# A one-core hybrid decoder layer: other load prices for the planner, small inverses head by head, one chain of k norms per head, and a new layout of the final norm

## The chip, the cores and the metric

One core of a Trainium2 chip runs the whole kernel. The metric is the device time of one execution in microseconds (us); the kernel before was run three times. The engines are TensorE (PE), VectorE (DVE), ScalarE (ACT), GpSimd (POOL) and SyncE (SP); SP issues all loads and stores here. PSUM has eight banks of 512 float32 columns, into which PE writes.

## What is computed

One layer and a final norm, batch 1, 1024 tokens, width 1024, all float32:

```python
h = rmsnorm(x, norm_mix_w);  proj = h @ W_in
qkv = silu(causal_conv4(qkv));  q, k = l2norm(q), l2norm(k)      # 4 heads of 128
o = gated_delta_rule_chunked(q, k, v, g, beta)                   # chunks of 64, I + A solved per chunk
gdn_out = rmsnorm(o) * silu(z)
lru_out = rg_lru(causal_conv4(lru_x)) * gelu(lru_gate)           # 512 channels, gates, scan over tokens
x = x + concat(gdn_out, lru_out) @ W_out
u = relu(rmsnorm(x) @ W1);  x = x + (u * u) @ W2                 # 4096 wide
return rmsnorm(x, final_norm_w)
```

## The kernel before

Activations are kept transposed, features on the partitions and tokens along the free axis, in two halves of 512 tokens. Each float32 product is three matmuls of split operands (`mm3`, line 439: high by high, high by low, low by high), so an operand costs a cast on ACT (the high part) and a subtraction on DVE (the low part).

**Stages.** PE works through: the first tiles with the input norm and the gates (to 45 us); the 28 tiles of the input projection, with the delta rule's heads and the recurrent unit's groups strewn between them (the mixer, to 408 us); the output projection (to 488); the first feed-forward product as seven Winograd products per pair of blocks (to 795); and the second, which has the four stages of `STAGES` (line 1250), products (1, 7), (6, 5), (2, 4) and (3). A stage walks over 16 column blocks in pairs; for each block `get2` (line 1263) loads tiles of W2 (`w2r`) and of the stored activations (`ur`), combines and splits them, and `mm3` adds to the stage's PSUM banks `p2`, eight for a stage of two products. At the end of a stage DVE or ACT reads each bank into the running sums `p1`, `u2`, `u3`, `p5`.

**Heads.** When a head's q and k tiles are there, `after_tile` (line 1028) records `decay`, `gd_k` (684) and `gd_q` (717) for each half: decay rows `DT` from a load `qg<-gcd`, the k norms (`sk`, `rk`, `cj`), the products `psA` and from them `U`. `invert32(h)` (739) then inverts the 32 x 32 diagonal blocks: SP copies U's blocks to DRAM and back as `N` (bn, N), POOL runs 31 steps of two operations (`tm`, `V`), SP copies the result to `Y` (bv, Y). `gd_inv` and `gd_scan` use it.

**Tail.** `normed` (1317) makes the final norm: sums of squares by matmuls into bank `n3p`, an inverse square root by `rsqrt` (485: a bit trick and three Newton steps on DVE), the factor broadcast to all partitions by PE into `n3b`, then a multiply for each of eight tiles into `ot`, and the store. It is called once for tokens 0 to 511, and for the other half in two quarters of 256 tokens (`end=True`), whose last products have 256 columns.

**Order.** Nothing runs as it is written. Every call is recorded as an operation with a due time (`pl.at`, `chain`) in the class `Plan`. `emit` (280) then plays the operations through with prices (`price`, 259): at each step it takes the operation that could start first, earliest due time first among those that can, and writes it to its engine. That fixes each engine's order, and it also fixes which buffer a tile gets: of the 84 slabs of 128 x 512 and of the eight banks, the one that in the played time came free last before the start. A real operation then waits for whichever engine last used that buffer. A load's price is its bytes at a rate, plus a constant to landing; `SLACK` is added before a mixer matmul counts as ready. Since all instructions are written out by one statement, all have the line L370.

```python
r.slot = max((x for x in sl if x[0] <= s), default=min(sl))
...
if e == "sy":
    free[e] = s + 0.45
    dma = max(dma, free[e] + 0.65) + c
    o.end = dma + 0.95
```

Of the kernel before, what the change touches and what calls it, by code (L numbers as in the profile page):

```python
# [9 lines left out]
AF = mybir.ActivationFunctionType  # L10
# [23 lines left out]
SLACK = 1.5  # L34
# [145 lines left out]
class Plan:  # L180
# [78 lines left out]
    def price(e, method, args, kw):  # L259
# [6 lines left out]
        if e == "sy":  # L266
            return n * shape[0] * 4 / 360e3
# [10 lines left out]
        return 0.15 + 0.0021 * n  # L278

    def emit(self, engines, caps):  # L280
# [62 lines left out]
        for _ in range(len(ops)):  # L343
# [15 lines left out]
            if e == "sy":  # L359
                free[e] = s + 0.45  # L360
                dma = max(dma, free[e] + 0.65) + c
                o.end = dma + 0.95
# [22 lines left out]
def layer(ctx: ExitStack, tc: tile.TileContext, xT, win, wba, prm, cst, wga, wgx, wout, w1, w2, out):  # L385
# [80 lines left out]
    gp.memset(onesd, 1.0 / D)  # L466
    with pl.at(due=-5000.0):
        ac.activation(out=one("load", [P, 1]), in_=onesd, func=AF.Exp)
# [16 lines left out]
    def rsqrt(y, x):  # L485

        t = small("rst", [P, 4], 3)[:, 0:x.shape[-1]]
        ve.tensor_scalar(out=y.bitcast(I32), in0=x.bitcast(I32), scalar1=1, scalar2=None, op0=ALU.logical_shift_right)
        ve.tensor_scalar(out=y.bitcast(I32), in0=y.bitcast(I32), scalar1=-1.0, scalar2=float(0x5f3759df), op0=ALU.mult, op1=ALU.add)
        for _ in range(3):  # L490
            ve.tensor_mul(out=t, in0=y, in1=y)
            ve.scalar_tensor_tensor(out=t, in0=t, scalar=-0.5, in1=x, op0=ALU.mult, op1=ALU.mult)
            ve.scalar_tensor_tensor(out=y, in0=t, scalar=1.5, in1=y, op0=ALU.add, op1=ALU.mult)
# [190 lines left out]
    def gd_k(h, hf):  # L684
        S = HD[h]
        c4 = slice(hf * 4, hf * 4 + 4)
# [7 lines left out]
        sk, cj = S["sk"][:, c4], S["cj"][:, c4]  # L694
        for c in range(4):
            cc = slice(c * P, (c + 1) * P)
            ac.activation(out=small("osq", [P, P], 2), in_=psK[:, cc], func=AF.Square, accum_out=S["sk"][:, hf * 4 + c:hf * 4 + c + 1])
            ac.activation(out=kd[:, cc], in_=psK[:, cc], func=AF.Copy, scale=d[:, c, P - 1:P])
        ve.tensor_scalar_add(out=sk, in0=sk, scalar1=EPS)
        rk = small("rk", [P, 4])  # L700
        rsqrt(rk, sk)
        ve.tensor_mul(out=cj, in0=rk, in1=G["beta"][:, h, c4])
        ve.tensor_mul(out=cj, in0=cj, in1=rk)
        ve.tensor_mul(out=sk, in0=sk, in1=rk)

        psA = bank("psA")
        with pl.unit(0.86):
            for c in range(4):
                ks = slice(c * P, (c + 1) * P)
                pe.matmul(psA[:, ks], lhsT=kT[:, ks], rhs=kT[:, ks], start=True, stop=True)  # L710
        U = S["U"][hf]
        for c in range(4):
            n = hf * 4 + c
            ve.scalar_tensor_tensor(out=U[:, c * P:(c + 1) * P], in0=psA[:, c * P:(c + 1) * P], scalar=S["cj"][:, n:n + 1],
                                    in1=S["DT"][hf][:, c * P:(c + 1) * P], op0=ALU.mult, op1=ALU.mult)

    def gd_q(h, hf):
# [16 lines left out]
        pn = S["pn"][:, hf * 4:hf * 4 + 4]  # L734
        for c in range(4):
            ac.activation(out=small("osq", [P, P], 2), in_=psQ[:, c * P:(c + 1) * P], func=AF.Square, accum_out=pn[:, c:c + 1])
        ve.tensor_scalar(out=pn, in0=pn, scalar1=EPS, scalar2=EPS * P, op0=ALU.add, op1=ALU.mult)
# [780 lines left out]
```

## Time and profile before

| | |
|---|---|
| runs, us | 1141.26, 1143.0, 1137.72; median 1141.26 |
| profiled execution | 1138.41 us, its span 1136.4 us (2.0 us lie around it) |
| PE busy | 1098.7 us, 97% of the span |
| DVE, ACT, POOL busy | 864.9 us (76%), 561.9 us (49%), 98.2 us (9%) |
| mean granted PE clock | 0.985 of full speed |

An engine's busy share is an average over stages. PE is pipelined, so a stretch of starts without gaps tells more than a busy time; a timeline row gives the start, the duration and, in brackets, the idle time ahead of it with what ended it.

### The profile page before, as it was taken

How to read it: one execution, taken by the hardware profiler on the slowest of the kernel's cores; microseconds unless marked ns; L12 is line 12 of the kernel's file. 1: busy time of each engine (PE TensorE's matmuls, PEld its weight loads, DVE VectorE, ACT ScalarE, POOL GpSimd, SP SyncE). 2: the span in 40 equal slices, each digit the busy share in tenths (PEclk: the TensorE clock that was granted, in tenths of full speed). 3: DMA queues.
4: the chain of work that ended last, by engine and by line, in shares of the span. 5: the costliest groups of instructions: out<-in, count | busy, mean ns of one | idle time of the engine just before them, and what ended most of it. 6: DMA issues, size and time to landing. Idle time of an engine off the chain costs nothing.

```text
span 1136.4 us, 16117 instructions
## 1 busy us (share of the span) xinstructions
PE 1098.7 (97%) x5439; PEld 903.7 (80%) x5439; DVE 864.9 (76%) x1730; ACT 561.9 (49%) x1143; POOL 98.2 (9%) x285
## 2 busy tenths in 40 slices
PE   9999899999999999999999999999999999799994
PEld 7788678787787878888888888888888788688884
DVE  7978486786769686698978788888765756865886
ACT  8578446354475865554333333334445434554432
POOL 0004826125000000000000000000000000000001
PEclk9999899999999999999999999999999999899997
DMA  6122312121111034424443434446755455476454
GB/s 232 38 72 60 93 41 68 28 62 40 46 37 38 19 129 147 150 93 167 176 175 131 166 141 159 147 158 222 242 193 200 154 178 204 162 237 210 166 177 149
DMA packets 88098, 150.79 MB, mean 133 GB/s; under 512 B 22312, under 2 KB 25040, under 8 KB 88016
## 3 DMA queue, kind: packets, MB, share of 16 engines
q1 hardware_dynamic: 88016, 149.77, 38.6%
q8 instruction: 43, 0.70, 0.3%
q14 instruction: 39, 0.32, 0.1%
HBM read 110.91 MB, written 38.82 MB: 132 GB/s over the span
## 4 chain that ended last, share of the span: by engine, by line
PE 75%; DVE 8%; POOL 8%; issue 3%; ACT 2%; DMA 2%; SPq 1%; DVEq 0%; POOLq 0%
PE p L370 27%; PE pf L370 27%; PE pj L370 8%; PE po L370 7%; POOL V L370 4%; POOL tm L370 4%; SPq L370 1%; DVE y L370 1%; PE pvs L370 1%; DVE ig L370 1%; ACT L370 1%; PE psr L370 1%; DVE ss L370 1%; PE psZ L370 1%; PE psO L370 1%
## 5 line engine op out<-in xcount | busy, mean ns | idle before, releaser
L370 PE MATMUL pj<-xh,w 128*128 128x512 f32 x704 | 248.4, 408 | 1.4 <-DVE S L370 0.7
L370 PEld LDWEIGHTS pj<-xh,w 128*128 128x128 f32 x704 | 133.7, 190 | 29.4 <-DVE S L370 1.1
L370 PE MATMUL pj<-xl,w 128*128 128x512 f32 x352 | 138.5, 394 | 0.0
L370 PE MATMUL po<-mxh,w 128*128 128x512 f32 x256 | 79.3, 390 | 0.4 <-ACT mxh L370 0.4
L370 DVE TENSOR_TENSOR w<-r,w 128x512 fp32r<-128x512 f32 (+1 forms) x62 | 59.0, 951 | 26.2 <-ACT w L370 25.8
L370 ACT ACTIVATE c<-c 128x512 f32<-128x512 f32 x64 | 40.1, 630 | 74.0 <-DVE c L370 74.0
L370 DVE SCALAR_TENSOR_TENSOR y<-p,pr,y 128x512 f32<-128x512 f32 (+3 forms) x96 | 72.0, 754 | 5.3 <-ACT y L370 4.4
L370 ACT CAST w<-r 128x512 fp32r<-128x512 f32 (+1 forms) x62 | 51.4, 830 | 49.1 <-PE pf L370 29.0
L370 POOL TENSOR_TENSOR r<-p__9746,n3rb 128x256 f32<-128x256 f32 x2 | 1.9, 974 | 850.8 <-DMA outT<-r 850.8
L370 PEld LDWEIGHTS pj<-xl,w 128*128 128x128 f32 x352 | 67.1, 190 | 10.2
L370 PEld LDWEIGHTS po<-mxh,w 128*128 128x128 f32 x256 | 48.0, 188 | 10.7 <-ACT mxh L370 0.8
L370 POOL TENSOR_TENSOR tm<-V,N 128x60 f32<-128x60 f32 (+24 forms) x124 | 43.6, 354 | 145.1 <-DMA N<-bn 110.0
L370 PE MATMUL po<-mxl,w 128*128 128x512 f32 x128 | 49.9, 390 | 1.2 <-DVE mxl L370 1.2
L370 POOL TENSOR_TENSOR V<-V,tm 128x60 f32<-128x60 f32 (+24 forms) x124 | 44.9, 365 | 8.3
L370 DVE SCALAR_TENSOR_TENSOR c<-c,n2B 128x512 f32<-128x512 f32 x64 | 43.7, 689 | 0.5
L370 ACT ACT_TABLE_LOAD x31 | 39.8, 1283 | 6.3 <-DVE y L370 3.7
L370 PE MATMUL pf<-B5h,w 128*128 128x512 f32 x128 | 42.4, 391 | 0.0
L370 PE MATMUL pf<-B6h,w 128*128 128x512 f32 x128 | 42.0, 389 | 0.0
L370 DVE TENSOR_TENSOR c<-pf,u 128x512 f32<-128x512 f32 x48 | 32.8, 688 | 0.8 <-PE pf L370 0.4
L370 PE MATMUL p<-u2h,v2h 128*128 128x512 f32 x64 | 25.8, 403 | 7.0 <-ACT u4h L370 7.0
L370 DVE TENSOR_TENSOR s<-w2r,s 128x512 f32<-128x512 f32 x16 | 11.1, 691 | 26.5 <-DMA w2r<-w 26.5
L370 PEld LDWEIGHTS po<-mxl,w 128*128 128x128 f32 x128 | 24.0, 188 | 6.5 <-DVE mxl L370 1.5
(513 smaller groups left out, 3025.6 us busy)
## 6 DMA issues: line engine op xcount, KB each, us to landing
w2r<-w SPq DMA_DIRECT2D x112, 256.0 KB, 3.4
ur<-ud SPq DMA_DIRECT2D x112, 256.0 KB, 5.1
r<-w SPq DMA_DIRECT2D x32, 512.0 KB, 3.6
ud<-c SPq DMA_DIRECT2D x64, 256.0 KB, 2.0
ud<-ut SPq DMA_DIRECT2D x48, 256.0 KB, 2.1
r<-win SPq DMA_DIRECT2D x22, 512.0 KB, 3.7
xraw<-xT SPq DMA_DIRECT2D x16, 256.0 KB, 5.3
r<-wout SPq DMA_DIRECT2D x8, 512.0 KB, 4.4
```

Source lines behind the costliest of these rows:

```text
L370: getattr(engines[e], method)(*[v.ap() if isinstance(v, View) else v for v in args], **{k: v.ap() if isinstance(v, View) else v for k, v i ...
```

## The change

- The planner's prices: a load's bytes at 300 instead of 360 GB/s, 2.0 us to landing instead of 0.95, a POOL operation 0.05 us dearer, a slack of 1.0 instead of 1.5 us. All orders, slabs and banks come out anew.
- `gd_k` makes no norms; a new `gd_u(h)` makes one chain for both halves of a head (8 columns), then both `psA` and `U`. The q sums get their addition once per head.
- `invert32(h)` may start only after the last POOL operation of head h-1's inverse.
- Final norm, both quarters: Sqrt on ACT with a bias and a DVE reciprocal and one Newton step in place of bit trick and three steps; an early Sqrt (`root`) on a scalar tile; the multiplies read the bank `n3b` itself, all on DVE, without ACT's copy `n3rb` and POOL's share. Outputs go through slabs in place of two buffers of 128 x 1024. The sum of squares of the finished tiles stands second in the list instead of first, and all eight last banks take block 14 first and then block 15.

```diff
--- before.py
+++ after.py
@@ -31,7 +31,8 @@
 LOOK = 4
-SLACK = 1.5
+SLACK = 1.0
+LAND = 2.0
 EPS = 1e-6
@@ -264,7 +265,7 @@
         if e == "sy":
-            return n * shape[0] * 4 / 360e3
+            return n * shape[0] * 4 / 300e3
         psum = any(v.root.tag == "m" for v in src)
@@ -275,7 +276,7 @@
             return 0.036 + 0.00083 * n
-        return 0.15 + 0.0021 * n
+        return 0.2 + 0.0021 * n
 
@@ -359,7 +360,7 @@
                 dma = max(dma, free[e] + 0.65) + c
-                o.end = dma + 0.95
+                o.end = dma + LAND
             else:
@@ -464,6 +465,8 @@
     gp.memset(onesd, 1.0 / D)
+    eps = one("eps", [P, 1])
+    gp.memset(eps, EPS)
     with pl.at(due=-5000.0):
@@ -484,13 +487,16 @@
 
-        t = small("rst", [P, 4], 3)[:, 0:x.shape[-1]]
         ve.tensor_scalar(out=y.bitcast(I32), in0=x.bitcast(I32), scalar1=1, scalar2=None, op0=ALU.logical_shift_right)
         for _ in range(3):
-            ve.tensor_mul(out=t, in0=y, in1=y)
-            ve.scalar_tensor_tensor(out=t, in0=t, scalar=-0.5, in1=x, op0=ALU.mult, op1=ALU.mult)
-            ve.scalar_tensor_tensor(out=y, in0=t, scalar=1.5, in1=y, op0=ALU.add, op1=ALU.mult)
+            newton(y, x)
+
+    def newton(y, x):
+        t = small("rst", [P, NC], 3)[:, 0:x.shape[-1]]
+        ve.tensor_mul(out=t, in0=y, in1=y)
+        ve.scalar_tensor_tensor(out=t, in0=t, scalar=-0.5, in1=x, op0=ALU.mult, op1=ALU.mult)
+        ve.scalar_tensor_tensor(out=y, in0=t, scalar=1.5, in1=y, op0=ALU.add, op1=ALU.mult)
 
@@ -683,7 +689,6 @@
         S = HD[h]
-        c4 = slice(hf * 4, hf * 4 + 4)
         d = b3(S["DT"][hf])
@@ -691,28 +696,33 @@
         kd = S["kd"][hf] = slab("kd")
-        sk, cj = S["sk"][:, c4], S["cj"][:, c4]
         for c in range(4):
             ac.activation(out=kd[:, cc], in_=psK[:, cc], func=AF.Copy, scale=d[:, c, P - 1:P])
+
+    def gd_u(h):
+
+        S = HD[h]
+        sk, cj = S["sk"], S["cj"]
         ve.tensor_scalar_add(out=sk, in0=sk, scalar1=EPS)
-        rk = small("rk", [P, 4])
+        rk = small("rk", [P, NC])
         rsqrt(rk, sk)
-        ve.tensor_mul(out=cj, in0=rk, in1=G["beta"][:, h, c4])
+        ve.tensor_mul(out=cj, in0=rk, in1=G["beta"][:, h, :])
         ve.tensor_mul(out=cj, in0=cj, in1=rk)
         ve.tensor_mul(out=sk, in0=sk, in1=rk)
-
-        psA = bank("psA")
-        with pl.unit(0.86):
+        for hf in range(2):
+            kT = store[4 + h, hf]
+            psA = bank("psA")
+            with pl.unit(0.86):
+                for c in range(4):
+                    ks = slice(c * P, (c + 1) * P)
+                    pe.matmul(psA[:, ks], lhsT=kT[:, ks], rhs=kT[:, ks], start=True, stop=True)
+            U = S["U"][hf]
             for c in range(4):
-                ks = slice(c * P, (c + 1) * P)
-                pe.matmul(psA[:, ks], lhsT=kT[:, ks], rhs=kT[:, ks], start=True, stop=True)
-        U = S["U"][hf]
-        for c in range(4):
-            n = hf * 4 + c
-            ve.scalar_tensor_tensor(out=U[:, c * P:(c + 1) * P], in0=psA[:, c * P:(c + 1) * P], scalar=S["cj"][:, n:n + 1],
-                                    in1=S["DT"][hf][:, c * P:(c + 1) * P], op0=ALU.mult, op1=ALU.mult)
+                n = hf * 4 + c
+                ve.scalar_tensor_tensor(out=U[:, c * P:(c + 1) * P], in0=psA[:, c * P:(c + 1) * P], scalar=cj[:, n:n + 1],
+                                        in1=S["DT"][hf][:, c * P:(c + 1) * P], op0=ALU.mult, op1=ALU.mult)
 
@@ -731,10 +741,12 @@
                 pe.transpose(psQ[:, c * P:(c + 1) * P], qT[:, c * P:(c + 1) * P], ident)
-        pn = S["pn"][:, hf * 4:hf * 4 + 4]
+        pn = S["pn"]
         for c in range(4):
-            ac.activation(out=small("osq", [P, P], 2), in_=psQ[:, c * P:(c + 1) * P], func=AF.Square, accum_out=pn[:, c:c + 1])
-        ve.tensor_scalar(out=pn, in0=pn, scalar1=EPS, scalar2=EPS * P, op0=ALU.add, op1=ALU.mult)
+            n = hf * 4 + c
+            ac.activation(out=small("osq", [P, P], 2), in_=psQ[:, c * P:(c + 1) * P], func=AF.Square, accum_out=pn[:, n:n + 1])
+        if hf == 1:
+            ve.tensor_scalar(out=pn, in0=pn, scalar1=EPS, scalar2=EPS * P, op0=ALU.add, op1=ALU.mult)
 
@@ -764,6 +776,7 @@
             gp.tensor_tensor(out=V[:, 0:r, m + 1:], in0=V[:, 0:r, m + 1:], in1=tv, op=ALU.subtract)
+        S["inv"] = pl.ops[-1]
         bv = pl.tile(dpool, [32, 8, 4, 32], F32, "bv", "bv", True)
@@ -1039,6 +1052,8 @@
                     with pl.at(due=t, gate=HD[h]["rowop"][1]):
+                        gd_u(h)
+                    with pl.at(due=t, gate=HD[h - 1]["inv"] if h else HD[h]["rowop"][1]):
                         invert32(h)
@@ -1314,7 +1329,7 @@
 
-    def normed(hf, X, parts, a, n, t, lead, end):
+    def normed(X, parts, a, n, t, lead, end):
 
@@ -1326,34 +1341,31 @@
             r, v = small("n3r", [P, 4])[:, 0:m], small("ms", [P, 4])[:, 0:m]
-            if one is not None:
+            if end:
+                for c in range(m):
+                    ac.activation(out=r[:, c:c + 1], in_=pn[c], func=AF.Sqrt, bias=eps)
+                    ve.tensor_scalar_add(out=v[:, c:c + 1], in0=pn[c], scalar1=EPS)
+                ve.reciprocal(out=r, in_=r)
+                newton(r, v)
+            else:
                 ve.tensor_scalar_add(out=v, in0=one[:, 0:m], scalar1=EPS)
-            else:
-                for c in range(m):
-                    ve.tensor_scalar_add(out=v[:, c:c + 1], in0=pn[c], scalar1=EPS)
-            rsqrt(r, v)
+                rsqrt(r, v)
             pb = bank("n3b")
                 rows(pb, r, m)
-            if end:
-                rb = slab("n3rb")[:, 0:n]
-                ac.copy(out=rb, in_=pb[:, 0:n])
-            g = T // n
+            g = 512 // n
             for j, d in enumerate(lead):
                 if j % g == 0:
-                    ot = raw_t("ot")
+                    ot = slab("ot")
                 y = ot[:, j % g * n:j % g * n + n]
                     ve.scalar_tensor_tensor(out=y, in0=X[d], scalar=par("fnw", d), in1=pb[:, 0:n], op0=ALU.mult, op1=ALU.mult)
-                elif j in (3, 5):
-                    gp.tensor_mul(out=y, in0=X[d], in1=rb)
                 else:
-                    ve.tensor_mul(out=y, in0=X[d], in1=rb)
-                k = 1 if end and j < 2 else 2
-                if (j + 1) % k == 0:
-                    b = lead[j + 1 - k]
-                    sy.dma_start(out=out[b * P:(b + k) * P, a:a + n].rearrange("(d p) t -> p d t", p=P),
-                                 in_=ot[:, (j + 1 - k) % g * n:(j % g + 1) * n].rearrange("p (d t) -> p d t", d=k))
+                    ve.tensor_tensor(out=y, in0=pb[:, 0:n], in1=X[d], op=ALU.mult)
+                if (j + 1) % g == 0:
+                    b = lead[j + 1 - g]
+                    sy.dma_start(out=out[b * P:(b + g) * P, a:a + n].rearrange("(d p) t -> p d t", p=P),
+                                 in_=ot.rearrange("p (d t) -> p d t", d=g))
 
@@ -1427,15 +1439,17 @@
                         plus(s1, y)
-            normed(0, [p1[d] for d in range(4)] + [u3[d] for d in range(4)], [(s1, t - 40)], 0, 512, t - 30, list(range(KT)), False)
+            normed([p1[d] for d in range(4)] + [u3[d] for d in range(4)], [(s1, t - 40)], 0, 512, t - 30, list(range(KT)), False)
 
     t = ts(3, NG - 2)
+    with pl.at(due=-1000.0, gate=seen[3 * NG + 4]):
+        ac.activation(out=one("root", [P, 1]), in_=onesd, func=AF.Sqrt, bias=eps)
     with chain(t - 60):
         qs = slice(o, o + 256)
-        parts = [(ss[:, qs], t)]
+        parts = []
         xs = {}
@@ -1448,8 +1462,9 @@
                 ac.activation(out=xs[d], in_=x, func=AF.Copy, scale=par("fnw", d))
+        parts.insert(1, (ss[:, qs], t))
         X = [xs[d] for d in range(4)] + [p5[d][:, qs] for d in range(4)]
-        normed(1, X, parts, 512 + o, 256, t + o / 50, [4, 5, 6, 7, 0, 1, 2, 3], True)
+        normed(X, parts, 512 + o, 256, t + o / 50, [4, 5, 6, 7, 0, 1, 2, 3], True)
```

How the order moves, at three places. **SP in stage 2 of the second feed-forward product**, the loads of blocks 12 and 13 (a row's brackets are the semaphores it waits for: DMA queues, and the engine that last used the buffer). Before:

```order
L370 DMA w2r_9347<-w2 128x512 [waits DMAHW6_49,DMAHW5_49,DVE_49]
L370 DMA w2r_9349<-w2 128x512 [waits DMAHW7_49]
L370 DMA ur_9354<-ud12_6_7559 128x512 [waits DMAHW0_49,PE_49]
L370 DMA ur_9359<-ud12_5_7539 128x512 [waits DMAHW1_49,PE_49]
L370 DMA w2r_9361<-w2 128x512 [waits DMAHW4_49,DMAHW2_49]
L370 DMA w2r_9366<-w2 128x512 [waits DMAHW3_49]
L370 DMA ur_9371<-ud13_6_7728 128x512
L370 DMA ur_9374<-ud13_5_7708 128x512
```

Now:

```order
L371 DMA w2r_9307<-w2 128x512 [waits DMAHW6_49,PE_49]
L371 DMA w2r_9311<-w2 128x512 [waits DMAHW7_49]
L371 DMA ur_9316<-ud12_6_7520 128x512 [waits DMAHW0_49,DVE_49]
L371 DMA ur_9321<-ud12_5_7480 128x512 [waits DMAHW5_49,DMAHW1_49,DVE_49]
L371 DMA w2r_9323<-w2 128x512 [waits DMAHW2_49]
L371 DMA w2r_9328<-w2 128x512 [waits DMAHW3_49]
L371 DMA ur_9333<-ud13_6_7689 128x512 [waits DMAHW4_49]
L371 DMA ur_9335<-ud13_5_7649 128x512
```

The first w2 load of the pair waited for DVE, and the u loads for PE. Now the w2 load waits for PE, and the first two u loads for DVE.

**SP at head 1 in the mixer**: gcd loads `qg`, block copies `bn` and `N` of the inverses, W_in tiles `r`. Before:

```order
L370 DMA r_1173<-win 128x1024 [waits DMAHW4_49,Activation_49]
L370 DMA qg_1206<-gcd_708 128x512 [waits DMAHW5_49]
L370 DMA bn_1223<-U1_0_1204 32x4x32 [waits DMAHW6_49,DVE_49]
L370 DMA bn_1223<-U1_0_1204 32x4x32 [waits DMAHW7_49]
L370 DMA bn_1223<-U1_0_1204 32x4x32 [waits DMAHW0_49]
L370 DMA bn_1223<-U1_0_1204 32x4x32 [waits DMAHW1_49]
L370 DMA bn_1223<-U1_1_1309 32x4x32 [waits DMAHW2_49,DVE_49]
L370 DMA bn_1223<-U1_1_1309 32x4x32 [waits DMAHW3_49]
L370 DMA bn_1223<-U1_1_1309 32x4x32 [waits DMAHW4_49]
L370 DMA bn_1223<-U1_1_1309 32x4x32 [waits DMAHW5_49]
L370 DMA qg_1353<-gcd_708 128x512 [waits DMAHW6_49,Pool_49]
L370 DMA r_1368<-win 128x1024 [waits DMAHW7_49,Activation_49]
```

Now:

```order
L371 DMA r_1070<-win 128x1024 [waits DMAHW4_49,Activation_49]
L371 DMA N0_1107<-bn_1027 32x512 [waits DMAHW5_49,DMAHW3_49,DMAHW6_49,DMAHW2_49,DMAHW7_49,DMAHW1_49,DMAHW0_49]
L371 DMA N0_1107<-bn_1027 32x512 x3
L371 DMA N1_1138<-bn_1027 32x512 [waits DVE_49,PE_49]
L371 DMA N1_1138<-bn_1027 32x512 x2
L371 DMA N1_1138<-bn_1027 32x512 [waits DMAHW4_49]
L371 DMA qg_1165<-gcd_714 128x512 [waits DMAHW5_49]
L371 DMA qg_1231<-gcd_714 128x512 [waits DMAHW6_49,DVE_49,PE_49]
L371 DMA r_1311<-win 128x1024 [waits DMAHW7_49]
L371 DMA r_1430<-win 128x1024 [waits DMAHW0_49,DVE_49]
L371 DMA bv_1477<-V_795 256x1x32 [waits DMAHW1_49,Pool_49]
```

Head 1's second load, qg_1353, stood behind its eight block copies and waited for POOL. Now both gcd loads, qg_1165 and qg_1231, stand behind head 0's N copies and ahead of every copy of head 1, and the second waits for DVE and PE.

**DVE in the tail** (`ms`, `n3r`, `rst`: norm chain; `r` or `ot`: outputs). Before, the end of the norm chain and the first outputs of the quarters:

```order
L370 SCALAR_TENSOR_TENSOR rst_11083<-rst_11083,ms_11074 128x2
L370 SCALAR_TENSOR_TENSOR n3r_11078<-rst_11083,n3r_11078 128x2
L370 SCALAR_TENSOR_TENSOR r_11102<-p7__8893,pr_75,n3b_10995 128x512
L370 SCALAR_TENSOR_TENSOR r_11102<-p7__8923,pr_75,n3b_10995 128x512
L370 TENSOR_TENSOR rst_11083<-n3r_11078 128x2
L370 SCALAR_TENSOR_TENSOR rst_11083<-rst_11083,ms_11074 128x2
L370 SCALAR_TENSOR_TENSOR n3r_11078<-rst_11083,n3r_11078 128x2
L370 TENSOR_TENSOR r_11116<-p5__9653,n3rb_11104 128x256
L370 TENSOR_TENSOR r_11116<-p5__9686,n3rb_11104 128x256
L370 TENSOR_TENSOR r_11116<-p5__9715,n3rb_11104 128x256
L370 TENSOR_TENSOR r_11124<-xf_10962,n3rb_11104 128x256
L370 TENSOR_TENSOR r_11124<-xf_10986,n3rb_11104 128x256
```

Now, the whole of the two chains and the first outputs:

```order
L371 TENSOR_SCALAR ms_11054<-n3p_11027 128x1
L371 TENSOR_SCALAR ms_11054<-n3p_11028 128x1
L371 RECIPROCAL n3r_11051<-n3r_11051 128x2
L371 TENSOR_TENSOR rst_11061<-n3r_11051 128x2
L371 RECIPROCAL n3r_11056<-n3r_11056 128x2
L371 SCALAR_TENSOR_TENSOR rst_11061<-rst_11061,ms_11024 128x2
L371 TENSOR_TENSOR rst_11065<-n3r_11056 128x2
L371 SCALAR_TENSOR_TENSOR n3r_11051<-rst_11061,n3r_11051 128x2
L371 SCALAR_TENSOR_TENSOR rst_11065<-rst_11065,ms_11054 128x2
L371 SCALAR_TENSOR_TENSOR n3r_11056<-rst_11065,n3r_11056 128x2
L371 TENSOR_TENSOR ot_11076<-n3b_11070,p5__9614 128x256
L371 TENSOR_TENSOR ot_11076<-n3b_11070,p5__9646 128x256
```

The first half's multiplies (`r_11102<-p7`) have left the tail, the two chains are seven instructions behind the sums, and the outputs read the bank n3b.

## Rows read from the trace of the kernel before

**Rows 1.** Windows by stage: stretch, its us, busy us (instructions) by engine, PEclk, DMA share, GB/s.

```profile
100.00:150.00 50.00, 46.45 (x279) 37.45 (x277) 30.33 (x75) 26.12 (x68) 43.07 (x125) 0.93 0.24 62
...
885.00:970.00 85.00, 85.00 (x376) 70.18 (x374) 53.35 (x83) 34.20 (x61) 0.00 (x0) 1.00 0.54 186
...
978.00:1064.00 86.00, 86.00 (x371) 70.78 (x371) 55.54 (x87) 40.71 (x67) 0.00 (x0) 0.97 0.61 208
```

**Rows 2.** PE's waits: tile and releaser, then us in total, times, longest us.

```profile
PE p L370 <- ACT u4h L370: 7.0, 1, 7.0
PE n3b L370 <- DVE n3r L370: 4.0, 2, 3.1
PE psV L370 <- ACT y L370: 3.5, 1, 3.5
PE wz L370 <- DVE wz L370: 1.5, 1, 1.5
```

**Rows 3.** Timeline of PE, 968 to 982 us: start, us, instruction, [idle before, releaser].

```profile
969.75 0.39 PE L370 MATMUL p<-u5h,v5l 128*128 128x512 f32 x1
977.18 0.76 PE L370 MATMUL p<-u2h,v2h 128*128 128x512 f32 x1 [7.04 <-ACT u4h L370]
...
980.73 0.63 PE L370 MATMUL p<-u4h,v4l 128*128 128x512 f32 x1
```

**Rows 4.** Timeline of DVE, 944 to 979 us, around the end of stage 2.

```profile
948.34 0.69 DVE L370 TENSOR_TENSOR s<-w2r,s 128x512 f32<-128x512 f32 x1 [2.92 <-DMA w2r<-w]
...
968.81 0.69 DVE L370 TENSOR_TENSOR u<-p,p__8820 128x512 f32<-128x512 f32 x1
...
976.34 0.69 DVE L370 TENSOR_TENSOR u<-p,p__8905 128x512 f32<-128x512 f32 x1
```

**Rows 5.** Timeline of SP, 933 to 959 us: two bursts of loads.

```profile
945.44 0.81 SPq L370 DMA_DIRECT2D w2r<-w  x2
...
957.29 0.81 SPq L370 DMA_DIRECT2D w2r<-w  x2
```

**Rows 6.** Timelines of SP, DVE and PE, 104 to 131 us, at head 1.

```profile
107.53 2.08 SPq L370 DMA_DIRECT2D bn<-U  x4
114.05 0.34 SPq L370 DMA_DIRECT2D qg<-gcd  x1
...
118.56 0.69 DVE L370 TENSOR_TENSOR DT<-qg,cs 128x512 f32<-128x512 f32 x1 [6.28 <-DMA qg<-gcd]
...
124.87 0.78 PE L370 MATMUL pj<-xh,w 128*128 128x512 f32 x1
...
129.71 0.74 PE L370 MATMUL pj<-xh,w 128*128 128x512 f32 x2
```

**Rows 7.** Timelines of POOL and SP, 170 to 212 us, inverse of head 2.

```profile
176.79 0.24 POOL L370 TENSOR_TENSOR tm<-V,N 128x31 f32<-128x31 f32 x1 [27.05 <-DVE y L370]
...
204.04 2.51 SPq L370 DMA_DIRECT2D bv<-V  x4
```

**Rows 8.** Timelines of PE, DVE and ACT, 1103 to 1137 us, the tail.

```profile
1107.27 0.28 PE L370 MATMUL p<-u3h,v3h 128*128 128x256 f32 x1
...
1111.23 0.42 DVE L370 TENSOR_TENSOR u<-p,u 128x256 f32<-128x256 f32 x1 [1.18 <-PE p L370]
...
1115.97 0.42 ACT L370 ACTIVATE sq<-u 128x256 f32<-128x256 f32 x1
...
1116.78 0.42 ACT L370 ACTIVATE sq<-u 128x256 f32<-128x256 f32 x1
...
1121.02 0.16 DVE L370 SCALAR_TENSOR_TENSOR n3r<-rst,n3r 128x2 f32<-128x2 f32 x1
...
1122.24 0.37 ACT L370 COPY n3rb<-n3b 128x256 f32<-128x256 f32 x1 [4.64 <-PE n3b L370]
...
1123.14 0.42 DVE L370 TENSOR_TENSOR r<-p__9653,n3rb 128x256 f32<-128x256 f32 x1 [0.18 <-DMA outT<-r]
...
1130.98 1.62 DVE L370 TENSOR_TENSOR r<-xf,n3rb 128x256 f32<-128x256 f32 x3 [0.68 <-DMA outT<-r]
```

## The prediction

> **What bounds the kernel now.** The matrix engine (PE) bounds it: the table ahead of this has it busy for 97% of the span. So I looked for where it is not, and at what clock it works. The windows by stage come first: stage 2 of the second feed-forward product is full, 376 matmuls in 85.00 us or 0.226 us each, while the mixer's stretch from 100 to 150 us and the stretch from 978 us run at a mean granted clock of 0.93 and 0.97 [rows 1]. Then PE's waits by releaser: three of them, 7.0, 4.0 (in two) and 3.5 us, lead the list, which goes on from 1.5 us down [rows 2]. The largest lies between stages 2 and 3, the second in the final norm, the third in the mixer at head 1. The timeline of each place says why. The sum below is made against the profiled execution, 1138.41 us; the median of the runs is 2.85 us above it.
>
> **Part 1, the load and slab plan at stage 2 to 3.** PE starts its last matmul of stage 2 at 969.75 and its next at 977.18, so 7.43 us for a step of 0.23: 7.2 us lost. From there to 980.73 eight steps take 3.55 us, 0.44 each, which is the lower of the two clock levels (1.2 GHz) after the idle stretch: 1.7 us more [rows 3]. What is awaited is a PSUM bank: in the built program stage 3's first product takes the bank of the last of stage 2's four outputs, and the vector engine (DVE) reads that bank only at 976.34, the thirteenth of a list that it began at 968.81 [rows 4]. DVE is late because of a ring. The first w2 load of each pair of column blocks takes a slab that DVE's last operation on the pair before gives back, and then DVE waits 2.92 us for that load [rows 4]. The bursts of loads start 11.85 us apart, where PE needs 48 x 0.226 = 10.8 us for a pair [rows 5]; over the stage's seven pairs DVE's lead shrinks by about 1 us each time, until the bank's reader is late. In the changed order, shown ahead, the two w2 loads of a pair wait for PE (which gave their slabs back pairs earlier), and only the two u loads behind them wait for DVE. Without the 2.92 us the ring takes about 8.9 us, less than PE's 10.8, so DVE keeps its lead. The bank is still that of the last output, and its read can't start before its last matmul, so PE still waits for one DVE instruction: 0.69 us [rows 4] and a signal each way, about 1.1 us. Term: 7.2 + 1.7 - 1.1 = **-7.8 us**; bounds 0 (DVE still late) and -8.9.
>
> The higher price for a byte and the 2.0 us for a landing change no duration on the chip; they only move loads earlier in the queue. [...]
>
> **Part 2, head 1's decay load.** The sync engine (SP) issues head 1's four block copies at 107.53, is through by 109.61, and issues nothing until 114.05, where the second gcd load goes out; it lands as DVE begins DT at 118.56, after an idle 6.28 us [rows 6]. That load waits for GpSimd (POOL), whose inverse of head 0 holds the slab it is to take. DT, its exponential and the silu of the next convolution tile stand in line behind, and PE waits 3.5 us for that silu [rows 2]. Then from 124.87 to 129.71 eleven starts take 4.84 us where 2.49 would do: 2.4 us more at the lower clock [rows 6]. In the changed order both gcd loads stand directly behind head 0's N copies, and the second waits for DVE and PE, not for POOL. Term: **-5.9 us**. Its bounds are 0, if another operation of head 1 is late there, and -8, if some waits of 1 us go with it.
>
> The rest of the mixer I cost at nothing. One k-norm chain of 8 columns in place of two of 4, and one addition on pn, take some 70 short DVE instructions away; the cover is that DVE has idle time there and PE does not wait for these chains. Where the cover is gone, PE waits for U; that would be a wait below the list's 1.5 us [rows 2]. The slack of 1.0 instead of 1.5 us puts PE's small products nearer to what they wait for, which can lengthen the small waits: first rival.
>
> **Part 3, the small inverses one by one.** POOL does the same instructions. Alone it takes 27.2 us for a head, from 176.79 to the copy out at 204.04 [rows 7]; with the copies in and out and the vector steps behind I count about 45 us from one head to the next (an estimate). From the place of each head's first product with its inverse in PE's new order, and PE's pace, the results are due 8 to 12 us after I expect them. Term: 0; the other end is the third rival.
>
> **Part 4, the tail.** Before, from the first 256-column matmul at 1107.27 to the end of the span at 1136.4: 29.1 us [rows 8]. In it lie the first half's eight multiplies, three Newton steps, an ACT copy of the broadcast norm, and DVE's waits for an output DMA to give back one of two buffers, the last of them 0.68 us [rows 8]. After, the first half's norm and outputs stand among stage 4's operations, and the outputs have slabs of their own. The chain that is left: 27 matmuls of 256 columns at half of 0.226 until the first output is whole, 3.1; its addition 0.42; then the scalar engine (ACT), with a square and a scaled copy for each of eight tiles, 0.81 us a pair, so the last square ends at 3.1 + 0.5 + 7 x 0.81 + 0.42 = 9.7. The sums' matmuls to 10.1; two Sqrt, the reciprocal and one Newton step, six short steps of 0.16 and a gap, to 11.3; from the last short step to the first reader of the broadcast 1.06 (1121.18 to 1122.24), so 12.4; sixteen multiplies, 0.42 each and overlapping a little, 6.2; then 3.8 from DVE's last instruction (1132.60) to the end [rows 8]. That is 22.4. The tail starts about 1.4 us later, since the first half's broadcast (eight 128-column matmuls, 1.0) and a short wait lie ahead of it now. Term: 23.8 - 29.1 = **-5.3 us**. Bounds: -2, if a table load or a slow short instruction falls into the chain, and -7.5, if the first quarter's multiplies start before the second's norm.
>
> The multiplies now read PSUM. The two nearest rows say that this costs nothing: u<-p,u with one operand in PSUM takes 0.42, r<-p,n3rb from SBUF 0.42 [rows 8]. The Trainium skill (VectorE: DVE Perf Modes, "Rules for kernel authors") says for elementwise work on matmul output to accept the plain rate from PSUM, or to copy to SBUF first where many operations follow, which speaks against dropping the copy. By the rows the sum stays; by the page the dropped copy would have been the better choice and the term smaller.
>
> **Sum.** -7.8 - 5.9 - 5.3 = -19.0 us: 1138.41 - 19.0 = 1119.4, and I say 1119.5.
>
> **Rivals.** First: the mixer's gain is given back. With less slack and the inverses moved, PE meets other waits in the projection; for it speaks that small waits from 1.5 us down stand there today [rows 2] and that a new order draws them anew; against it, that only the one load waits for POOL. The price is 5.9 us (1125), or with new waits as large again about 1131 to 1136. Chance 0.2. Second: the wait between stages stays, because the loads are late for another reason (the u loads behind, or the bursts' rate) and the bank's reader is now fourteenth in DVE's list. 1119.4 + 7.8 = 1127. For it speaks that the bank rule is unchanged; against it the ring's sums. Chance 0.13. Third, on the other side: the serial inverses come too late. Each head's copies in wait for the previous head's last POOL operation. If a head takes 55 us rather than 45, the lag grows by 10 us a head: 40 at the fourth, less its 12 of margin, so PE stands about 28 us at head 3's products and then runs some us at the lower clock: about 1149. It decides from some 48 us a head. For it speaks that before, heads 0 and 1 ran side by side; against it, 27.2 us on POOL and the dues in the new order. Chance 0.07.
>
> **Numbers.** The forecast has 0.57 (1113 to 1123), the rivals 0.2, 0.13 and 0.07, and 0.03 is left for mishaps that cancel the gain. About 0.5%, 5.7 us, is what a measurement can tell from no change: below 1135.6 is faster, above 1147 slower. Faster: 0.57 + 0.13 + 0.13 from the first rival's lower part = 0.83. Same: 0.07 + 0.03 - 0.01 = 0.09. Slower: 0.07 + 0.01 = 0.08. The range reaches down to the three terms at their far bounds (1138.4 - 8.9 - 8 - 7.5 = 1114) and some of the mixer's smaller waits, and up over the first two rivals together (1119.4 + 5.9 + 7.8 = 1133) and the upper part of the first: 1107 to 1137.
>
> **What would show it.** Right: PE's wait between stages 2 and 3 is 1 to 1.5 us and the mean clock there 1.00; no DVE wait of 2.9 us per pair before w2 operations in stage 2; no wait of psV on a silu near 120 us; from the first 256-column matmul to the end 22 to 23 us, with no DVE wait on an output. Wrong: a PE wait over 3 us on psP or psZ in the mixer (the inverses), a burst distance over 10.8 us in stage 2, or an ACT table load behind the last square.

## The result and the profile after

The changed kernel takes 1111.2 us (median of 4 runs, 1110.96 to 1114.6) against 1142.13 us beside it: a ratio of 0.9743, 95% interval 0.971 to 0.9776, so 2.6% faster. The forecast was 1119.5 us, range 1107 to 1137. Its profiled span is 1109.4 us against 1136.4, 27.0 us less, where the sum of the prediction had 19.0.

Where the 27.0 us went, by the starts of the first matmul of each stage on PE's timeline (the names are the matmul's output; e9 is the changed kernel run again later):

| stretch, us | before | changed | difference | e9 | forecast |
|---|---|---|---|---|---|
| start to first projection (pj) | 41.0 | 42.7 | +1.6 | 42.3 | 0 |
| mixer, to the output projection (po) | 357.5 | 346.4 | -11.0 | 342.9 | -5.9 |
| po, first product pf, stage 1 of p | 484.0 | 483.2 | -0.8 | 483.5 | 0 |
| stage 2 | 94.7 | 87.05 | -7.65 | 87.07 | -6.1 |
| stage 3 | 91.06 | 87.07 | -4.0 | 87.06 | -1.7 |
| stage 4 to the first 256-column matmul | 39.03 | 40.16 | +1.1 | 40.19 | +1.4 |
| tail | 29.1 | 22.8 | -6.3 | 23.4 | -6.7 |

PE's waits by releaser in the changed kernel, the head of the list (us in total, times, longest), against [rows 2]:

```profile
PE psP L371 <- DVE S L371: 1.6, 1, 1.6
PE po L371 <- DVE mxl L371: 1.5, 1, 1.5
PE wz L371 <- DVE wz L371: 1.5, 1, 1.5
PE psP L371 <- DVE YP L371: 1.1, 1, 1.1
PE n3b L371 <- DVE rst L371: 1.1, 1, 1.1
```

The 7.0 us and the 3.5 us are gone, n3b is down from 4.0 to 1.1, and a tile that had not been in the list ahead of the prediction leads it: psP, the first product with a head's inverse.

PE's timeline of the changed kernel at stage 2 to 3 (start, us, instruction), which answers [rows 3]:

```profile
959.11 0.39 PE L371 MATMUL p<-u5h,v5l 128*128 128x512 f32 x1
959.34 0.39 PE L371 MATMUL p<-u2h,v2h 128*128 128x512 f32 x1
```

There is no wait at all. DVE starts to read the awaited bank 0.98 us ahead of it. SP's bursts come 10.88 us apart ([rows 5] had 11.85), which is PE's own pace for a pair here (87.05 / 8), and DVE waits for no w2 load in stage 2 any more:

```profile
958.36 0.68 DVE L371 TENSOR_TENSOR u<-p,p__8862 128x512 f32<-128x512 f32 x1
```

```profile
926.21 0.81 SPq L371 DMA_DIRECT2D w2r<-w  x2
937.09 0.81 SPq L371 DMA_DIRECT2D w2r<-w  x2
```

The tail, on PE, ACT and DVE: first 256-column matmul, last square, first and last outputs, which answer [rows 8].

```profile
1086.57 0.28 PE L371 MATMUL p<-u3h,v3h 128*128 128x256 f32 x1
```

```profile
1096.72 0.40 ACT L371 ACTIVATE sq<-u 128x256 f32<-128x256 f32 x1
```

```profile
1100.11 0.42 DVE L371 TENSOR_TENSOR ot<-n3b,p__9614 128x256 f32<-128x256 f32 x1 [1.06 <-PE n3b L371]
...
1104.10 1.40 DVE L371 TENSOR_TENSOR ot<-n3b,xf 128x256 f32<-128x256 f32 x4
```

The last square ends 10.55 us after the first 256-column matmul (9.7 in the forecast), the first output starts at 13.5 (12.4), the last output ends at 18.9 (18.6) and the span at 22.8 (22.4). No DVE wait on an output is left.

### The profile page after: what moved, and what is told of

It is laid out like the page before. It is cut to its first block, busy times and chain, and to the rows that moved or that the text cites. A ratio compares the mean times of both kernels' runs of the same rounds, so it can differ in the third digit from the quotient of the medians.

```text
span 1109.4 us, 15927 instructions
## 1 busy us (share of the span) xinstructions
PE 1089.9 (98%) x5439; PEld 898.4 (81%) x5439; DVE 855.8 (77%) x1656; ACT 559.0 (50%) x1144; POOL 101.2 (9%) x282
## 4 chain that ended last, share of the span: by engine, by line
PE 81%; DVE 5%; POOL 5%; ACT 3%; issue 2%; SPq 2%; DMA 1%; DVEq 0%; POOLq 0%; ACTq 0%
PE p L371 28%; PE pf L371 28%; PE pj L371 11%; PE po L371 7%; POOL V L371 2%; POOL tm L371 2%; SPq L371 2%; PE pvs L371 1%; DVE y L371 1%; PE psr L371 1%; PE psO L371 1%; DVE ig L371 1%; PE psba L371 1%; ACT rg L371 1%; PE psZ L371 1%
## 5 line engine op out<-in xcount | busy, mean ns | idle before, releaser
L371 POOL TENSOR_TENSOR tm<-V,N 128x60 f32<-128x60 f32 (+24 forms) x124 | 46.6, 376 | 133.1 <-DMA N<-bn 91.8
L371 POOL TENSOR_TENSOR V<-V,tm 128x60 f32<-128x60 f32 (+24 forms) x124 | 47.8, 385 | 9.7
L371 DVE TENSOR_TENSOR p<-pj,n1B 128x512 f32<-128x512 f32 x28 | 19.2, 686 | 17.5 <-PE pj L371 17.4
L371 ACT CAST v6h<-s 128x512 fp32r<-128x512 f32 x16 | 10.0, 623 | 40.2 <-DVE s L371 40.2
L371 PEld LDWEIGHTS pf<-B5h,w 128*128 128x128 f32 x128 | 24.0, 188 | 6.8 <-DVE c L371 1.9
```

The source lines that it names most:

```text
L371: getattr(engines[e], method)(*[v.ap() if isinstance(v, View) else v for v in args], **{k: v.ap() if isinstance(v, View) else v for k, v i ...
```

## The experiments

Each run shows its median against runs of the kernel before on the same chip. "Order the same" means that every engine's instructions stand in the order of the kernel before, word for word, and only slabs differ.

**e1, only the slab of the w2 tiles (order the same).**

```diff
-                    r.slot = max((x for x in sl if x[0] <= s), default=min(sl))
+                    r.slot = min(sl) if r.nm == "w2r" else max((x for x in sl if x[0] <= s), default=min(sl))
```

> The kernel before, with one rule changed: a w2r tile takes the slab that has been free longest, not the one that came free last. The order of every engine's instructions stays word for word; only which slab a tile gets, and so what a load waits for. Theory (ring through DVE's last slab): the 2.9 us waits of DVE for w2r in stage 2 go, bursts of loads follow PE's 10.8 us, PE's wait of 7.0 us at stage 2 to 3 and the lower clock behind it go: 9 to 10.5 us off the time, and nothing elsewhere. Rival (loads late for their own length, or the bank's reader being far down DVE's list decides): 0 to 2 us off.

1128.13 us against 1138.54, ratio 0.9919 (0.9897 to 0.9941). In PE's timeline stage 3 follows stage 2 without a wait; in DVE's, the awaited bank is read at 969.01, where [rows 4] have 976.34:

```profile
969.94 0.39 PE L370 MATMUL p<-u5h,v5l 128*128 128x512 f32 x1
970.17 0.39 PE L370 MATMUL p<-u2h,v2h 128*128 128x512 f32 x1
```

```profile
969.01 0.69 DVE L370 TENSOR_TENSOR u<-p,p__8905 128x512 f32<-128x512 f32 x1
```

DVE's waits for w2 loads from 885 us to the end of stage 2 (us in total, times, longest), before and in e1:

```profile
DVE s L370 <- DMA w2r<-w: 19.3, 9, 3.2
```

```profile
DVE s L370 <- DMA w2r<-w: 1.8, 3, 0.7
```

Stage 2 takes 87.04 us (94.7 before) and stage 3 88.05 (91.06): 10.7 us, where the medians differ by 10.4; the mixer (358.9, 357.5 before) and the tail (28.5, 29.1) differ by no more than single profiles do. With the same order on every engine, the ring through DVE's last slab is shown as the cause of the 7.0 us wait and of the lower clock behind it.

**e2, only the slab of the gcd loads (order the same).** The same edit with `r.nm == "qg"`.

> The kernel before, with the same rule for qg tiles alone; the order of all engines stays word for word, and head 1's second gcd load no longer waits for POOL. Theory: DVE's 6.28 us before DT and PE's 3.5 us wait for the silu near 120 us go, with the lower clock behind them: 5.5 to 6.5 us off. Rival (another operation of head 1 is late there, the block copies or DT's exponential): 0 to 2 us off.

1138.6 us against 1138.54, ratio 1.0003 (0.9989 to 1.0017): nothing. The mixer of its profile is no shorter (359.6 us, 357.5 before). The theory of the prediction's second part fell. The load is early now and DVE's wait of 6.28 us is gone, but PE's timeline has three waits in place of one:

```profile
116.36 0.66 PE L370 MATMUL psV<-cs,y 128*128 128x128 f32 x4 [1.82 <-ACT y L370]
...
130.49 0.50 PE L370 MATMUL pj<-xh,w 128*128 128x512 f32 x1 [1.92 <-ACT vs L370]
...
137.69 0.44 PE L370 MATMUL psP<-YT,U 32*32 32x32 f32 x16 [2.14 <-DVE YT L370]
```

1.82 + 1.92 + 2.14 = 5.9 us. Two of them end on a tile of ACT that has taken one of POOL's slabs in turn (ACT's timeline):

```profile
113.64 0.72 ACT L370 ACTIVATE y<-p,pr 128x512 f32<-128x512 f32 x1 [3.45 <-POOL tm L370]
...
129.30 1.14 ACT L370 ACTIVATE vs<-psV,sk 128x128 f32<-128x128 f32 x4 [5.45 <-POOL tm L370]
```

The third, psP, waits for the inverse of head 0 itself.

**e3, only the three prices.** 300 GB/s, 2.0 us, 0.2 for POOL, as in the diff ahead of the prediction.

> The kernel before with the planner's three prices of the change alone (300 GB/s, 2.0 us to landing, POOL 0.2); slack, norms, inverses and tail as before. Theory: the prices alone give the new slabs, so both the wait at stage 2 to 3 and the one at head 1 go: 13 to 17 us off. Rival (slabs are a draw that falls out otherwise with each order): one of the two waits stays, 0 to 9 us off.

1124.06 us, ratio 0.9873 (0.9858 to 0.9889). By the starts of the stages: start +1.6, mixer 353.1 (-4.3), stage 2 87.06 (-7.6), stage 3 88.08 (-3.0), tail 29.07. So 14.5 us came where 13 to 17 were expected, but they are not the sum of the two waits: the mixer gave 4.3 us. The prices alone free the ring, and they cost the 1.6 us at the start, which neither e4 (41.3 to the first projection) nor e6 (41.3) has.

**e4, only the final norm.** The hunks on `newton`, `eps`, `normed`, `root` and the last loop alone.

> The kernel before with the final norm of the change alone (Sqrt on ACT, one Newton step, no ACT copy and no POOL multiplies, slabs for the outputs, block 14 before 15). Theory: the tail from the first 256-column matmul to the end falls from 29.1 to about 22.8 us and about 1 us comes ahead of it: 5 us off, the waits at head 1 and at stage 2 to 3 stay. Rival (the tail was already covered by the transfers): under 2 us off.

1132.76 us, ratio 0.9952 (0.9935 to 0.9968). The tail falls from 29.1 to 22.5 us, stage 4 rises from 39.0 to 41.8; PE still waits 6.1 us at stage 2 to 3 and 3.6 us for the silu. As expected, except that stage 4 rises by 2.8 us where about 1 was expected.

**e5, POOL's slabs given out 10 us later (order the same).** After e2: are the slabs of the inverses the cause, whoever takes them?

```diff
-                    slots[r.tag].append((r.end + 0.2, r.slot[1]))
+                    slots[r.tag].append((r.end + (0.2 if r.nm not in ("N0", "N1", "V", "tm") else 10.0), r.slot[1]))
```

> The kernel before, with one rule changed: the planner counts a slab of the inverses (N0, N1, V, tm) as free 10 us after the played end instead of 0.2 us. The order of every engine stays word for word; other tiles no longer get these slabs at once. Theory, after the qg run: the mixer's waits come from tiles that take a slab which POOL in truth gives back later than the planner played (some 24 us of idle time of DVE and ACT end on POOL, its copies or the gcd load in the kernel before), and moving one tile only hands the wait on; so with all of them gone the mixer loses 5 to 9 us, 0.5 to 0.8% of the time. Rival (the inverses' results themselves are late, whoever has the slabs): 0 to 2 us.

1138.4 us against 1139.23, ratio 0.9995 (0.9977 to 1.0013): the rival holds. No DVE or ACT operation between 60 and 300 us waits for POOL any more, nor PE for the silu at 120 us, and all of it comes back in one wait, at head 0's psP. First PE's timeline of e5, then of the kernel before, then DVE's transpose of the inverse (YT) in the two:

```profile
138.33 0.64 PE L370 MATMUL psP<-YT,U 32*32 32x32 f32 x16 [6.48 <-DVE YT L370]
```

```profile
137.66 0.44 PE L370 MATMUL psP<-YT,U 32*32 32x32 f32 x16
```

```profile
137.84 0.45 DVE L370 STREAM_TRANSPOSE YT<-Y 128x256 f32<-128x256 f32 x1 [8.28 <-DMA Y<-bv]
```

```profile
136.47 0.45 DVE L370 STREAM_TRANSPOSE YT<-Y 128x256 f32<-128x256 f32 x1 [0.92 <-DMA Y<-bv]
```

PE meets psP of head 0 at 137.66 in the kernel before, 137.69 in e2 and 138.33 in e5; counted from the first projection matmul that is 96.62, 96.70 and 96.71 us (e1, which has the same order too, 95.97). This moment is set by the inverse (YT waits for the copy `Y<-bv`), and the earlier waits only shift where PE idles ahead of it. In the kernel before, the 3.5 us at 120 and the lower clock behind them use up just the time that PE would have waited for YT: psP itself shows no wait.

**e6, only the inverses one by one.** The gate of the diff and `S["inv"]`, in the kernel before.

> The kernel before with the inverses one by one alone (head h's copies and POOL operations after head h-1's last POOL operation). Theory: POOL's times in the plan come nearer to the truth, so fewer tiles wait for it, but later inverses cost PE waits at psP of heads 0 and 1 as in the changed kernel (1 to 2 us each): 0 to 4 us off. Rival of the prediction (the chain of the four heads comes too late): 5 to 28 us slower.

1144.58 us, ratio 1.0054 (1.0037 to 1.007): 5.3 us slower, at the edge of the third rival's range and against my theory. psP of head 0 moved up in PE's order, to 321 projection matmuls (333 before), and PE waits there, where DVE's transpose YT has waited 10.09 us for the copy to Y and its next operation, p, stands between:

```profile
136.55 0.64 PE L370 MATMUL psP<-YT,U 32*32 32x32 f32 x16 [5.65 <-DVE p L370]
```

By this product e6 has lost only some 1.4 us (95.3 us from the first projection matmul with 12 matmuls fewer ahead of it, 2.7 us of work, against 96.6). The rest comes later in the mixer, where PE waits 1.69 us at psP of head 1 and the granted clock is 0.86 from 175 to 200 us; it is not taken apart further.

**e7, only POOL's part gated.** The changed kernel, with `gate=HD[h]["rowop"][1]` for `invert32` and `pl.gate = HD[h - 1]["inv"]` ahead of its loop.

> The changed kernel, but only POOL's operations of head h wait for head h-1's inverse; the copies to N may go ahead. In the changed kernel they start after it, stand between the result copies bv and Y of the head before, and POOL idles 15 us between heads. Theory: Y of heads 0 and 1 lands 3 to 15 us earlier, PE's three waits at psP (0.7, 1.1 and 1.6 us, with the lower clock after the last) go: 4 to 6 us off the changed kernel's 1111. Rival (a new draw of slabs gives the gain back): within 2 us of it.

1119.8 us, ratio 0.9823 (0.98 to 0.9846): some 9 us slower than the changed kernel, so this theory fell. The waits at head 0's psP went, as expected, and POOL ran heads 0 and 1 without a gap; but the new order puts products of one head's inverse among those of another's scan around 220 us, where PE waits 0.5, 1.1 and 1.7 us for DVE within 4.5 us and the granted clock falls (window row of e7, columns as in [rows 1]; the changed kernel has 1.00 there):

```profile
200.00:250.00 50.00, 46.64 (x336) 39.97 (x336) 36.39 (x116) 20.85 (x79) 6.13 (x20) 0.90 0.18 50
```

**e8, three scaled copies on DVE.** The changed kernel, with

```diff
-                ac.activation(out=xs[d], in_=x, func=AF.Copy, scale=par("fnw", d))
+                if o and d >= 1:
+                    ve.tensor_scalar(out=xs[d], in0=x, scalar1=par("fnw", d), scalar2=None, op0=ALU.mult)
+                else:
+                    ac.activation(out=xs[d], in_=x, func=AF.Copy, scale=par("fnw", d))
```

> The changed kernel, with the scaled copy xf of the last three tiles of the second quarter on DVE, which idles 2.7 us there, instead of ACT. Theory (ACT's square and scaled copy, eight pairs, set the tail): the last square ends three times 0.4 us earlier, 1.0 to 1.5 us off the changed kernel's 1111. Rival (PE's last matmuls and additions set it): 0 to 0.4 us.

1107.27 us, ratio 0.9716 (0.9698 to 0.9734); the changed kernel has 0.9743 and, in e9, 0.9747 (0.9729 to 0.9765). The intervals overlap, so a gain of 0.3% is likely and not settled. The first output starts 12.2 us after the first 256-column matmul instead of 13.5, as expected; in the profiled execution 1.1 us of it is lost in the stores, one of which took 1605 ns to issue. The stores' line and their landing times, e8 and then the changed kernel:

```profile
L371 SPq DMA_DIRECT2D outT<-ot x8: 384/450/1605, 1096.2 to 1101.6; - x8
...
DMA to landing us min/median/max: 2.9/3.4/4.0
```

```profile
L371 SPq DMA_DIRECT2D outT<-ot x8: 372/372/397, 1100.9 to 1105.5; - x8
...
DMA to landing us min/median/max: 2.2/2.6/2.9
```

**e9, the changed kernel again.**

> The changed kernel itself once more, beside the next three, as their base on this chip. Expected: ratio to the kernel before 0.971 to 0.978, with waits of PE at psP of heads 0 and 1 that differ by a us or two from the first profile, since the inverse's result and PE arrive there almost together.

1109.7 us against 1138.83, ratio 0.9747 (0.9729 to 0.9765). The first profile had these waits at psP of heads 0 and 1; e9 has none at head 0 and 1.06 us at head 1, and its mixer is 3.5 us shorter (342.9):

```profile
140.69 0.44 PE L371 MATMUL psP<-YT,U 32*32 32x32 f32 x16 [0.67 <-DVE YT L371]
...
143.74 0.44 PE L371 MATMUL psP<-YT,U 32*32 32x32 f32 x16 [1.13 <-DVE YP L371]
```

```profile
189.39 0.44 PE L371 MATMUL psP<-YT,U 32*32 32x32 f32 x16 [1.64 <-DVE S L371]
```

PE and the inverse meet within 2 us there. The copy out of head 0's inverse starts at 131.00 us in the first profile and at 129.08 in e9, and of the 3.5 us 2.0 are idle time of PE and 1.5 its busy time, the granted clock being 0.97 from 150 to 200 us in the first and 1.00 in e9. So on this meeting the mixer's time hangs in these two profiles.

**e10, without the gate between inverses.** The changed kernel with `gate=HD[h]["rowop"][1]` for `invert32`.

> The changed kernel without the gate between the heads' inverses: heads 0 and 1 share POOL again. Theory, now: what counts in the mixer is how far behind in PE's order a head's first product with its inverse (psP) stands, against the time its inverse takes. PE meets psP of head 0 after 375 projection matmuls here, 360 in the changed kernel, 333 in the one before; head 0's inverse is through POOL some 20 us later when it shares it. So PE waits 2 to 6 us at psP of head 0: 2 to 6 us over the changed kernel, at about 1114 to 1118. Rival (the gate is not needed once the prices are true): within 2 us of it.

1113.28 us, ratio 0.9781 (0.9763 to 0.98), 3.6 us over e9, inside the 2 to 6 us that were expected; but not by the wait that was. The copy out of head 0's inverse starts at 134.36 us, 5.3 us after e9's and not 20, and PE waits at no first psP of heads 0 and 1, only once at a later one of head 0:

```profile
155.44 0.68 PE L371 MATMUL psP<-YT,U 64*64 64x64 f32 x8 [0.87 <-ACT YT L371]
```

The mixer takes 346.6 us instead of 342.9, of which only 0.9 us is idle time of PE (3.4 against 2.5); the rest is longer busy time, spread over the mixer. In the new order the gate is worth some 0.3%, and why is not shown.

**e11, the old slack.** The changed kernel with `SLACK = 1.5`.

> The changed kernel with the slack at 1.5 us again. Prediction's first rival: the smaller slack costs PE waits in the mixer, so the old slack gives 1 to 5 us off. Theory: it doesn't matter where PE's waits come from inverses: within 3 us of the changed kernel, psP of head 0 at 363 projection matmuls instead of 360.

1118.35 us, ratio 0.9823 (0.9807 to 0.9839): 8.6 us slower than e9. Both the theory and the rival are wrong: the smaller slack gained. The mixer takes 349.4 us, and most of the excess lies between 220 and 231 us (3.2 us of idle time, granted clock 0.84), where one head's scan stands in PE's order without projection matmuls between. PE's timeline, and DVE's at the same place: a convolution of 1.53 us stands ahead of `vh` on DVE.

```profile
224.54 0.49 PE L371 MATMUL pvs<-vs,Y 128*128 128x128 f32 x2 [0.58 <-DVE vs L371]
226.25 0.49 PE L371 MATMUL pvs<-vh,kd 128*128 128x128 f32 x2 [1.22 <-DVE vh L371]
```

```profile
224.40 1.53 DVE L371 SCALAR_TENSOR_TENSOR y<-p,pr,y 128x512 f32<-128x512 f32 x2
225.85 0.35 DVE L371 TENSOR_SCALAR vh<-pvs,cj 128x128 f32<-128x128 f32 x1
```

e3 (slack 1.5) and e7 (slack 1.0) have such a cluster too, so it comes with an order and not with the slack as such.

**e12, the copies to Y ahead of the next head's.** e8 with `S["inv"] = pl.ops[-1]` set behind the copies to Y. In the changed kernel SP's timeline has the next head's copies first:

```profile
131.00 2.60 SPq L371 DMA_DIRECT2D bv<-V  x4
133.65 3.46 SPq L371 DMA_DIRECT2D bn<-U  x7
137.15 3.76 SPq L371 DMA_DIRECT2D Y<-bv  x8
```

> The changed kernel with two edits: a head's inverse starts after the last copy to Y of the head before (in the changed kernel the next head's block copies stand between bv and Y and hold Y up by 3.5 us), and three scaled copies of the last quarter on DVE. psP of the four heads stands after 360, 510, 633 and 768 projection matmuls (360, 492, 600 and 723 in the changed kernel). Theory: no PE wait at any psP, 2 to 4 us off the changed kernel, about 1105 to 1109 on this chip. Rival: the scans at the end of the mixer come later with the fourth head and PE waits at the output projection, no gain.

1110.96 us, ratio 0.9758 (0.9738 to 0.9778): no gain over e9, and 0.4% behind e8, which has the same edit to the tail. PE waits at no psP, as expected, and the tail takes 21.3 us (e9 23.4); but the mixer takes 345.9 (342.9), with waits of 1.1, 0.9 and 0.8 us at other products (`pj` twice, `pvs` once). The rival's wait at the output projection is no longer than e9's (1.2 us, 1.5), so its "no gain" came without its cause.

## Why the prediction was right or wrong

**Direction and bound.** Right: 2.6% faster, inside the range, 8.3 us below the number. In the profiles the 27.0 us are -10.65 in part 1 (-7.8 forecast), -11.0 in the mixer (-5.9), -6.2 in part 4 (-5.3), +1.6 at the start and -0.8 between the mixer and stage 2 (both 0). PE's waits in the three places all went, but the one in the mixer was not worth its length (part 2). That the mixer gained all the same, and more than the term, was luck as far as the prediction goes: nothing in its reasons gives it.

**Part 1** ("Term -7.8 us") was right in its mechanism (e1, e3) and too small: -10.65 us, of which 7.65 in stage 2 and 3.0 in stage 3. Two sizes were off. The rest wait of 1.1 us isn't there: I took the awaited bank for the last that stage 2 finishes, but one more output, which ACT reads, stands behind it on PE, 6 matmuls or 1.4 us, and DVE's read fits into them. And I ended the stretch at the lower clock with the row at 980.73, the last one that I had looked at. PE's timeline of the kernel before goes on at that clock:

```profile
982.86 0.60 PE L370 MATMUL p<-u2l,v2h 128*128 128x512 f32 x1
983.28 0.41 PE L370 MATMUL p<-u2h,v2l 128*128 128x512 f32 x1
```

From 977.18 to 983.28 are 14 steps in 6.10 us where 3.17 would do, 2.9 us instead of 1.7.

**Part 2** ("Term -5.9 us") named the wrong cause. The step that failed is "PE waits 3.5 us for that silu", read as a wait whose removal is a gain. e2 took the late load away and e5 every wait on POOL's slabs, with the same order, and neither gained: up to there the bound is the inverse of head 0, on POOL and through its copies to `Y`, and psP, where PE needs it. The view that says so was at hand and I did not use it: the chain that ended last, in the page's fourth part, before and after:

```profile
PE 75%; DVE 8%; POOL 8%; issue 3%; ACT 2%; DMA 2%; SPq 1%; DVEq 0%; POOLq 0%
```

```profile
PE 81%; DVE 5%; POOL 5%; ACT 3%; issue 2%; SPq 2%; DMA 1%; DVEq 0%; POOLq 0%; ACTq 0%
```

8% of 1136 us is some 91 us of POOL in a chain that I had put down to PE. The share says where to look and is no price: e9, the changed kernel again, has 2%. In the changed order psP of head 0 stands behind 360 projection matmuls instead of 333, 27 x 0.227 = 6.1 us more projection work ahead of a result that comes no earlier (its transpose starts at 140.10, 136.47 before). With 12 smaller products of some 0.11 us each that stand ahead of it too, 7.4 us more work is done in 1.4 us more (98.0 us from the first projection matmul to psP, 96.6 before): about 6 of the 11.0 us are won up to there, which is the size of the term. In e3 psP stands behind 381 projection matmuls, and about 5 us are won up to it. No run moved psP alone, so it is argued from e2, e3, e5 and the orders, not shown by itself. The other 5 us come behind this product (in e3 nothing does), where the waits fall out otherwise in each order (e7, e10, e11, e12: 346 to 353 us). The whole mixer, before and now (stretch, its us, PE's busy us):

```profile
41.04:398.49 357.45, 347.08 (x2081) 285.26 (x2079) 265.43 (x709) 215.69 (x554) 90.81 (x262) 0.99 0.16 48
```

```profile
42.67:389.11 346.44, 341.90 (x2081) 282.94 (x2079) 260.50 (x649) 215.09 (x557) 99.16 (x269) 1.00 0.17 50
```

PE's idle time falls from 10.4 to 4.5 us, and its busy time for the same products by 5.2 us. The k norms, costed at nothing, have no run of their own (DVE's instructions in the mixer fall from 709 to 649). By the medians the prices alone (e3), the norm at the end (e4) and the gate (e6) make -14.5, -5.8 and +5.3 us, -14.9 together, and the whole change -29.1 (e9): about half comes only with the slack, the k norms and the order that all make together, and what each of these is worth stays open.

**Part 3** ("Term: 0", inverses) was no zero: alone the gate costs 5.3 us (e6), in the new order it gains some 3.6 (e10). The pace was sized well: the copies out of the four inverses start 46.4 to 46.7 us apart (45 in the estimate). The margin of 8 to 12 us was not there: in the first profile PE waits 0.67 and 1.64 us at the first psP of heads 0 and 1.

**Part 4** ("Term -5.3 us") was right: the tail -6.3, the 1.1 us of the first half's norm in stage 4, and 1.0 us less of it in stage 3, where I had not looked for it (e1 and e3 still have it there): together -6.2. Dropping the copy for reads of PSUM cost nothing that shows: an output takes 0.42 us from n3b, as from SBUF [rows 8]. The Trainium skill (VectorE: DVE Perf Modes, "Rules for kernel authors") leaves both ways open, to read PSUM at the plain rate or to copy first where many operations follow; with eight reads of each bank the trace here shows no price for doing without the copy.

**The start**, 1.6 us slower, was not in the sum; e3 shows that the prices make it.

**Rivals.** The first (the mixer gives its gain back through the smaller slack) was wrong in its sign: e11 loses 8.6 us with the old slack. The second did not come. The third's mechanism is real (e6), a fifth of its price, and in the new order it leaves only waits of 0.7 to 1.6 us at psP.

## What to carry to other kernels

A wait in a timeline is worth its length only if nothing later waits for the same late thing: take the chain of waits first, and ask what PE meets next. Where a planner hands out buffers, a price in its sums that is too low makes no instruction slower but lets tiles take buffers that come back late; a run that keeps the order and changes only the buffer tells the two apart. Follow a stretch at a lower clock to the row where it ends before pricing it.

## What was not expected

- Three kernels with one order and different slabs meet at the same product within 0.7 us (137.66, 137.69, 138.33), although their waits ahead of it are 3.5, 3.7 and 0 us.
- The changed kernel's mixer took 346.4 us in one profile and 342.9 in another, with one order and the same slabs; e8, whose mixer is the same too, took 342.9.
- One of e8's eight last stores took 1605 ns to issue on SP, where the median is 450 ns there and 372 ns in the changed kernel; why is open.
